# Layer B's attention: in every second unit the twelve products of the output projection move ahead of the unit's value products

## Chip, cores and metric

The kernel runs on one core of one Trainium2 chip. The metric is device microseconds of one execution, as a median over runs; a profile is one further execution, recorded by the hardware profiler.

## What is computed

The reference is a two-layer decoder trunk on x of shape (1, 2048, 1024) in float32. Layer A is causal attention with forget gates. Layer B, which the change touches, is a sliding-window attention over keys and values that are shared by groups of heads, followed by a gate and an output projection:

```python
q, gate = jnp.split(u @ w_in_b[j], [WIDTH_B], axis=-1)
q = partial_rope(rmsnorm(q.reshape(b, s, N_Q_HEADS_B, HEAD_DIM), qnorm_b_g[j]), positions)
o = swa_sink_attention(q, k_shared, v_shared, sinks[j]).reshape(b, s, WIDTH_B)
h = h + (o * jax.nn.silu(gate)) @ w_out_b[j]
```

In `swa_sink_attention` each block of 128 queries sees its own and the previous block of 128 keys through a band mask, with one learned sink logit per head in the softmax. There are 16 query heads and 4 key/value heads, so 4 query heads share one.

## The kernel before

Each float32 matrix product is made of products of high and low parts, three for a projection (high by high, high by low, low by high).

`attention_b` cuts the attention into 64 units: 16 blocks of 128 queries, and in each block the 4 key/value heads g = 0 to 3. A unit passes through a software pipeline, one stage per step n of the loop `for n in range(N + V_LAG_B)`:

- *scores*, of unit n: eight products (L1302) into one of two PSUM tiles b2. VectorE lays the mask over them (L1314), puts in the sink (L1315) and takes the maxima (L1318, tile nm); ScalarE makes the exponentials and their sums (L1321, four per unit, tile st).
- *norm_weights*, of unit n - 1: VectorE's reciprocal (L1330), GpSimd's multiplication (L1331).
- *weights_t*, of unit n - 3: four transposes on TensorE (L349) into the one PSUM tile fl; ScalarE copies the high part (L1346), VectorE makes the residue (L1347), and GpSimd masks both (L1350). The results lie in two buffers by turns.
- *differences*, once a block, when n % 4 is 1: GpSimd subtracts the previous block's values from the block's (L1360, L1362), ScalarE makes the high part (L1364), GpSimd the residue (L1365).
- *values*, of unit n - 4: four products (L1381) into one of two PSUM tiles pa; ScalarE copies the lower half (L1388, tile wr), VectorE adds twice (L1391) and multiplies by the gate (L1395), then ScalarE makes the high part (L1397) and VectorE the residue (L1398). These two are one operand of the output projection.

The output projection (`project`) is a generator that issues one product (L1451) at each call. A half block is 128 rows by 512 columns: 24 products into the single PSUM tile pb, then VectorE adds the residual (L1457) and SyncE stores it (L1458). There are 32 half blocks, 768 products, and the loop takes 12 of them per unit, 8 units behind the scores: so a half block begins in an even unit and is complete at the end of an odd one. `feed` takes them in portions, six ahead of *values* and six after it. In the first units of this part the weights of the projection are split as well (L1431 on ScalarE, L1432 on VectorE).

The order in which the code issues the steps is not kept as written: a scheduler places the instructions on each engine, and it has a different result on ScalarE, VectorE, GpSimd and SyncE when the order of the calls changes. On every engine instructions then run in the order of its queue, and a wait holds everything behind it. SyncE's queue holds all the loads and stores: the block's keys (L1276, L1279), queries (L1275), values (L1288), gates (L1292), and the residual's rows for each half block (L1446).

The main loop of the pipeline is printed here with the functions around it.

Of the kernel before, what the change touches and what calls it, by code (L numbers as in the profile page):

```python
# [77 lines left out]
O_LAG_B = 8  # L78
# [6 lines left out]
FEED_2 = 6  # L85
# [66 lines left out]
class Trunk:  # L152
# [1103 lines left out]
    def attention_b(self, w_out, res, dst):  # L1256
# [27 lines left out]
        def load_v(i):  # L1284

            ts_ = slice(i * P, (i + 1) * P)
            v = self.sb(("qn", "qn", "rows")[i % 3], [P, NKV, P], F32R)
            nc.sync.dma_start(  # L1288
                out=f_(v), in_=d["vb"][:, ts_, :].rearrange("g t e -> t g e")
            )  # L1290
            g = yg[:, 2 + i % 2, :].rearrange("p (c t) -> p c t", t=P)
            nc.sync.dma_start(out=g, in_=d["gtb"][:, ts_].rearrange("(c p) t -> p c t", p=P))  # L1292
            blk[i][3:5] = v, g

        def scores(u):
            i, g = units[u]
            ka, k2, qa, _, _, w = blk[i]

            ps = self.ps("b2", [P, G, 2 * P])
            for h in range(G):  # L1300
                for j, k in enumerate((ka, k2)):
                    nc.tensor.matmul(  # L1302
                        ps[:, h, 2 * P - w :], qa[:, g * G + h, :], k[:, g, :w],
                        start=j == 0, stop=j == 1,
                    )


            lg = ps[:, :, P:]
            if i == 0:
                m = self.band[:, 0].unsqueeze(1).to_broadcast([P, G, P])  # L1310
                nc.vector.tensor_tensor(lg, lg, m, ALU.add)
            else:
                m = self.band[:, 1].bitcast(I16).unsqueeze(1).to_broadcast([P, G, P])
                nc.vector.copy_predicated(lg, m, ps[:, :, :P])  # L1314
            nc.vector.tensor_copy(ps[:, :, P - 1], self.sink[:, g * G : (g + 1) * G])  # L1315
            lg = ps[:, :, P - 1 :]
            nm, rs = (self.sb(x, [P, G], bufs=6) for x in ("nm", "rs"))
            nc.vector.tensor_reduce(nm, lg, AX.X, ALU.max, negate=True)  # L1318
            pf = self.sb("st", [P, G, P + 1])
            for h in range(G):  # L1320
                nc.scalar.activation(  # L1321
                    pf[:, h], lg[:, h], AF.Exp, bias=nm[:, h : h + 1],
                    accum_out=rs[:, h : h + 1],
                )
            st[u] = pf[:, :, 1:], rs

        def norm_weights(u):

            pf, rs = st[u]
            self.tc.keep_in_program_order(nc.vector.reciprocal(rs, rs))  # L1330
            nc.gpsimd.tensor_tensor(  # L1331
                pf, pf, rs.unsqueeze(2).to_broadcast([P, G, P]), ALU.mult
            )
            st[u] = pf

        def weights_t(u):


            i, g = units[u]
            pf = st[u]  # L1340
            ps = self.ps("fl", [P, G, P])
            for h in range(G):
                self.flip(ps[:, h, :], pf[:, h])
            both, own = (php[:, u % 2, k] for k in range(2))
            ph, pl = (both[:, k] for k in range(2))
            nc.scalar.copy(ph, ps)  # L1346
            nc.vector.tensor_tensor(pl, ps, f_(ph), ALU.subtract)  # L1347
            if i:
                tri = self.tri.unsqueeze(1).to_broadcast([P, 2 * G, P])
                nc.gpsimd.tensor_tensor(  # L1350
                    own.rearrange("p k h q -> p (k h) q"),
                    f_(both).rearrange("p k h q -> p (k h) q"), tri, ALU.mult,
                )
            st[u] = (ph, pl, own[:, 0], own[:, 1])

        def differences(i):

            v, before = f_(blk[i][3]), f_(blk[i - 1][3])
            t = self.sb("wl", [P, NKV, P])
            nc.gpsimd.tensor_tensor(t, v, before, ALU.subtract)  # L1360
            t_ = t[:, :, :HD]
            nc.gpsimd.tensor_tensor(t_, t_, t[:, :, HD:], ALU.add)  # L1362
            dv = self.sb("wh", [P, NKV, P], F32R)
            nc.scalar.copy(dv[:, :, :HD], t_)  # L1364
            nc.gpsimd.tensor_tensor(dv[:, :, HD:], t_, f_(dv[:, :, :HD]), ALU.subtract)  # L1365
            dvs[i] = dv

        def values(u):


            i, g = units[u]
            ph, pl, oh, ol = st.pop(u)
            if i:
                v, dv = blk[i - 1][3], dvs[i]
                terms = ((v, ph), (v, pl), (dv, oh), (dv, ol))
            else:
                v = blk[i][3]
                terms = ((v, ph), (v, pl))
            pv = self.ps("pa", [P, G, P])
            for n_, (v, src) in enumerate(terms):  # L1380
                nc.tensor.matmul(  # L1381
                    pv.rearrange("p h q -> p (h q)"), v[:, g, :],
                    src.rearrange("p h q -> p (h q)"),
                    start=n_ == 0, stop=n_ == len(terms) - 1,
                )

            cr = self.sb("wr", [HD, G, P])
            nc.scalar.copy(cr, pv[HD:])  # L1388
            y = pv[:, 1::2, :]
            for s in (1, 0):  # L1390
                nc.vector.tensor_tensor(  # L1391
                    y[s * HD : (s + 1) * HD], pv[:HD, s::2, :], cr[:, s::2, :], ALU.add
                )
            pr = slice(g * G // 2, (g + 1) * G // 2)
            nc.vector.tensor_tensor(y, y, blk[i][4][:, pr, :], ALU.mult)  # L1395
            yh, yl = (yt(i, k, pr) for k in range(2))
            nc.scalar.copy(yh, y)  # L1397
            nc.vector.tensor_tensor(yl, y, f_(yh), ALU.subtract)  # L1398
# [16 lines left out]
        def weight_load(j):  # L1415
            half, t = 1 - j // 4, j % 4 * 2
            raws[j] = self.sb("wr", [P, 2, CH])
            nc.sync.dma_start(
                out=raws[j],
                in_=w_out[t * P : (t + 2) * P, half * CH : (half + 1) * CH].rearrange(  # L1420
                    "(k p) c -> p k c", p=P
                ),
            )

        def weight_split(j):
            half, t = 1 - j // 4, j % 4 * 2
            if t % 4 == 0:
                W[half][t // 4] = self.sb("big", [P, 2, 4, CH], F32R)
            h, lo = (W[half][t // 4][:, k, t % 4 : t % 4 + 2, :] for k in range(2))
            raw = raws.pop(j)  # L1430
            nc.scalar.copy(h, raw)  # L1431
            nc.vector.tensor_tensor(lo, raw, f_(h), ALU.subtract)  # L1432
# [30 lines left out]
        def feed(n):  # L1463
            nonlocal fed
            while fed < min(n, total):
                next(filler, None)
                fed += 1

        per = total // N
        for n in range(N + V_LAG_B):  # L1470
            if n < N:
                scores(n)
            if 0 < n <= N:
                norm_weights(n - 1)
            if n == T_LAG_B:
                php = self.sb("big", [P, 2, 2, 2, G, P], F32R)
            if n == V_LAG_B + NKV:
                odd += [[self.sb(t, [P, 4, P], F32R) for _ in range(2)] for t in ("wh", "wl")]
            if 0 <= n - B_SPLIT_AT < NDT:
                weight_split(n - B_SPLIT_AT)  # L1480
            if 0 <= n + 1 - B_SPLIT_AT < NDT:
                weight_load(n + 1 - B_SPLIT_AT)
            o = (n - O_LAG_B) * per
            feed(o + FEED_1)
            if n % NKV == 1 and NKV < n < N:
                differences(n // NKV)
            if 0 <= n - T_LAG_B < N:
                weights_t(n - T_LAG_B)
            feed(o + FEED_2)
            if 0 <= n - V_LAG_B < N:  # L1490
                values(n - V_LAG_B)
            feed(o + per)
            if n < N:
                i, g = units[n]
                if g == NKV - 2 and i + 1 < NTB:
                    load(i + 1)
                if g == NKV - 1 and i + 1 < NTB:
                    load_v(i + 1)
            yield
# [121 lines left out]
```

## Time and profile before

| | us |
|---|---|
| median of 3 runs | 2443.16 |
| lowest, highest | 2442.53, 2444.26 |
| profiled execution, its time | 2441.85 |
| profiled execution, span from the first to the last instruction | 2440.1 |

| engine | busy us | share of the span |
|---|---|---|
| TensorE (PE) | 2408.3 | 99% |
| TensorE's weight loads (PEld) | 2025.6 | 83% |
| VectorE (DVE) | 1728.7 | 71% |
| ScalarE (ACT) | 1258.6 | 52% |
| GpSimd (POOL) | 998.5 | 41% |

TensorE ran at a granted clock of 0.999. In layer B's attention, from about 2117 us to the end, the rows of the profile name a line of the kernel, an engine, an operation and its tiles, output before inputs ("pb<-big" is written to pb and reads big). An idle time in square brackets stands with what ended it. Matmul records are given with a modelled end, so on TensorE the distance from one start to the next is the surer measure.

### The profile page before, as it was taken

How to read it: one execution, taken by the hardware profiler on the slowest of the kernel's cores; microseconds unless marked ns; L12 is line 12 of the kernel's file. 1: busy time of each engine (PE TensorE's matmuls, PEld its weight loads, DVE VectorE, ACT ScalarE, POOL GpSimd, SP SyncE). 2: the span in 40 equal slices, each digit the busy share in tenths (PEclk: the TensorE clock that was granted, in tenths of full speed). 3: DMA queues.
4: the chain of work that ended last, by engine and by line, in shares of the span. 5: the costliest groups of instructions: out<-in, count | busy, mean ns of one | idle time of the engine just before them, and what ended most of it. 6: DMA issues, size and time to landing. Idle time of an engine off the chain costs nothing.

```text
span 2440.1 us, 36268 instructions
## 1 busy us (share of the span) xinstructions
PE 2408.3 (99%) x11952; PEld 2025.6 (83%) x11952; DVE 1728.7 (71%) x4098; ACT 1258.6 (52%) x2504; POOL 998.5 (41%) x643
## 2 busy tenths in 40 slices
PE   8999999999999999999999999999999999999999
PEld 6788899987888788878888878888888888888887
DVE  7656667735989888888888866556666523777776
ACT  5433324323878778777877761135422312555554
POOL 0000000011878777777778862200011000377775
PEclk9999999999999999999999999999999999999999
DMA  5656555677654755566465649975433415555552
GB/s 182 208 167 183 157 154 168 197 232 236 173 167 128 204 159 148 148 195 177 131 183 175 176 139 310 294 247 163 126 92 116 138 65 166 177 178 181 178 181 74
DMA packets 351516, 419.24 MB, mean 172 GB/s; under 512 B 64928, under 2 KB 248256, under 8 KB 345152
## 3 DMA queue, kind: packets, MB, share of 16 engines
q1 hardware_dynamic: 351328, 416.92, 57.2%
q8 instruction: 95, 1.56, 0.3%
q14 instruction: 93, 0.76, 0.1%
HBM read 265.29 MB, written 151.40 MB: 171 GB/s over the span
## 4 chain that ended last, share of the span: by engine, by line
PE 86%; DVE 4%; DMA 4%; ACT 2%; issue 1%; POOL 1%; SPq 1%; ACTq 0%; DVEq 0%; POOLq 0%
PE b L759 27%; PE pa L1021 10%; PE pb L1061 7%; PE b L1238 5%; PE sc L979 5%; PE sc L978 5%; PE pb L1451 5%; PE mx L933 5%; PE pb L722 3%; PE b L722 3%; PE pa L1381 2%; PE b L1302 2%; DMA wr<-wg 1%; PE pa L349 1%; PE pb L349 1%
## 5 line engine op out<-in xcount | busy, mean ns | idle before, releaser
L759 PE MATMUL b<-wh,big 128*128 128x512 f32 (+3 forms) x2560 | 774.4, 375 | 8.9 <-ACT wh L486 8.5
L997 POOL TENSOR_TENSOR big<-st,big 128x1024 fp32r<-128x1024 f32 (+1 forms) x320 | 655.3, 2067 | 246.4 <-ACT big L996 154.9
L759 PEld LDWEIGHTS b<-wh,big 128*128 128x128 f32 x2560 | 472.3, 189 | 81.3 <-ACT wh L486 10.7
L759 PE MATMUL b<-wl,big 128*128 128x512 f32 (+3 forms) x1280 | 475.0, 371 | 1.7 <-DVE wl L487 1.6
L1006 DVE TENSOR_TENSOR ac<-ac,st 128x512 f32<-128x512 f32 (+3 forms) x576 | 352.3, 612 | 55.1 <-ACT st L993 29.3
L993 ACT ACTIVATE st<-sc 128x512 f32<-128x512 f32 (+1 forms) x512 | 273.1, 582 | 127.5 <-PE sc L979 59.5
L1021 PE MATMUL pa<-big 128*128 128x512 f32 (+3 forms) x1280 | 318.7, 365 | 1.0 <-POOL big L997 1.0
L996 ACT CAST big<-st 128x1024 fp32r<-128x1024 f32 (+1 forms) x320 | 295.2, 923 | 8.3
L759 PEld LDWEIGHTS b<-wl,big 128*128 128x128 f32 x1280 | 242.0, 189 | 37.8 <-DVE wl L487 5.5
L1021 PEld LDWEIGHTS pa<-big 128*128 128x128 f32 x1280 | 229.5, 190 | 40.4 <-POOL big L997 3.0
L946 DVE TENSOR_REDUCE mt<-mx 128x1 f32<-128x384 f32 (+1 forms) x360 | 213.9, 597 | 30.5 <-PE mx L933 28.3
L495 ACT ACTIVATE sq<-b,r 128x512 f32<-128x512 f32 (+2 forms) x128 | 77.7, 607 | 302.5 <-PE b L759 299.6
L978 PE MATMUL sc<-big 128*128 128x512 f32 (+3 forms) x640 | 232.8, 368 | 0.1
L979 PE MATMUL sc<-big 67*128 67x512 f32 (+3 forms) x640 | 229.4, 367 | 0.0
L933 PE MATMUL mx<-big 66*128 66x512 f32 (+2 forms) x600 | 224.6, 379 | 0.2
L1061 PE MATMUL pb<-wh,wr 128*128 128x512 f32 x488 | 178.8, 399 | 6.7 <-DMA wr<-wg 6.7
L497 DVE TENSOR_REDUCE sm<-sq 128x8 f32<-128x512 f32 (+2 forms) x128 | 74.9, 585 | 139.4 <-ACT sq L495 139.2
L859 POOL MEMSET rot<- 128x512 bf16 x1 | 0.5, 524 | 421.5 <-PE pb L349 421.5
L1350 POOL TENSOR_TENSOR big<-big,tri 128x1024 fp32r<-128x1024 f32 x60 | 143.8, 2397 | 67.4 <-DVE big L1347 62.5
L941 DVE CUSTOM_DVE_ANT_0 mx<-mx,rot 128x384 f32<-128x384 f32 (+2 forms) x240 | 146.8, 616 | 19.4 <-PE mx L933 18.4
L978 PEld LDWEIGHTS sc<-big 128*128 128x128 f32 x640 | 121.9, 190 | 21.6 <-DVE st L542 0.5
L979 PEld LDWEIGHTS sc<-big 67*128 67x128 f32 x640 | 122.1, 191 | 19.4
(281 smaller groups left out, 4120.5 us busy)
## 6 DMA issues: line engine op xcount, KB each, us to landing
wr<-wg SPq DMA_DIRECT2D x62, 512.0 KB
va<-st SPq DMA_DIRECT2D x32, 512.0 KB
ka<-st SPq DMA_DIRECT2D x64, 256.0 KB
ut<-big SPq DMA_DIRECT2D x16, 1024.0 KB
big<-ka SPq DMA_DIRECT2D x16, 1024.0 KB
big<-qa SPq DMA_DIRECT2D x16, 1024.0 KB
qb<-st SPq DMA_DIRECT2D x64, 256.0 KB
big<-qb SPq DMA_DIRECT2D x16, 1024.0 KB
```

The source lines that it names most:

```text
L759: nc.tensor.matmul(ps[:, :n], u[tb // 4][:, dt, us], W[k][dt], start=(dt == 0 and i == 0), stop=(dt == NDT - 1 and i == 2),)
L933: mm = nc.tensor.matmul(ps, qb[:66, i * P : (i + 1) * P], kb[:66, k0:k1], start=True, stop=True,)
L941: nc.vector.tensor_tensor_reduce(out=ps, in0=ps, in1=mask_m[:, 512 - w :], scale=1.0, scalar=NEG, op0=ALU.add, op1=ALU.max, accum_out=f_(o),)
L946: nc.vector.reduce_max(o, ps, axis=AX.X)
L978: nc.tensor.matmul(o, ka[:, ks], qa[:, qs], start=not (last and n_), stop=False)
L979: nc.tensor.matmul(o, kb[:, ks], qb[:, qs], start=False, stop=not diag)
L993: nc.scalar.activation(pf[:, off : off + w], ps[:, :w], AF.Exp, scale=HD**-0.5)
L996: nc.scalar.copy(ph[:, :tw], pf[:, :tw])
L997: nc.gpsimd.tensor_tensor(pl[:, :tw], pf[:, :tw], f_(ph[:, :tw]), ALU.subtract)
L1006: nc.vector.tensor_tensor(a_, a_, pf[:, off : off + w], ALU.add)
L1021: nc.tensor.matmul(pv[:, q0 : q0 + w], v[:, k, :], src[:, off : off + w], start=(p == 0 and n_ == 0 and i == 0), stop=(last and n_ == 1 an ...
L1061: nc.tensor.matmul(ps, w[:, dt // 2 % 2, wk, dt % 2, :], us[dt][uk], start=(dt == 0 and i == 0), stop=(dt == NDT - 1 and i == 2),)
```

## The change

In odd units (those that complete a half block) the second portion is fed whole, ahead of `values`; the call behind `values` then has nothing left to issue. In even units nothing is altered. The number of products and their order among themselves stay the same.

```diff
@@ -1486,7 +1486,7 @@
                 differences(n // NKV)
             if 0 <= n - T_LAG_B < N:
                 weights_t(n - T_LAG_B)
-            feed(o + FEED_2)
+            feed(o + (per if (n - O_LAG_B) % 2 else FEED_2))
             if 0 <= n - V_LAG_B < N:
                 values(n - V_LAG_B)
             feed(o + per)
```

`per` is 12, `FEED_2` is 6, `O_LAG_B` is 8. What it does to the order on three engines follows; a minus stands before what was there, a plus before what is there now.

TensorE, in an odd unit of the steady part: scores, transposes, projection (pb), value products (pa), and the next unit's scores.

```order
 L1302 MATMUL b_21565<-big 128x256 x8
 L349 MATMUL fl<-ident,st 128x128 x4
-L1451 MATMUL pb<-big 128x512 x6
+L1451 MATMUL pb<-big 128x512 x12
 L1381 MATMUL pa<-big,rows 128x512 x2
 L1381 MATMUL pa<-big,wh 128x512 x2
-L1451 MATMUL pb<-big 128x512 x6
 L1302 MATMUL b_21626<-big 128x256 x8
```

The last six products of the half block have changed places with the four value products. From the third block of the projection to the last the order on VectorE and ScalarE is the same as before.

ScalarE, in the first units of the projection, where the weights are split (L1431): copies of value sums (L1388), exponentials (L1321), copies of transposed weights (L1346), high parts (L1397, L1364).

```order
 L1346 CAST big<-fl 128x512
 L1397 CAST wh<-pa 128x256
-L1388 COPY wr<-pa 64x512
 L1321 ACTIVATE st,rs<-b_21086,nm 128x129 x4
 L1364 CAST wh<-wl 128x4x64
+L1388 COPY wr<-pa 64x512
 L1431 CAST big<-wr 128x1024
-L1397 CAST wh<-pa 128x256
-L1346 CAST big<-fl 128x512
 L1321 ACTIVATE st,rs<-b_21151,nm 128x129 x4
-L1388 COPY wr<-pa 64x512
+L1346 CAST big<-fl 128x512
```

The copy L1388 has moved behind L1364, and the copy of the transposed weights (L1346) behind the next four exponentials. On VectorE the addition L1457 of the first half block has moved ahead of a sum L1391 in these units, and on GpSimd the differences of the next block (L1360, L1362) stand one L1350 earlier.

SyncE, in a steady block, before:

```order
L1276 DMA big<-kb 128x4x256
L1275 DMA big<-qb 128x16x128
L1288 DMA rows<-vb 128x4x128
L1458 DMA out_h<-sq 128x512
L1279 DMA big<-kb 64x4x256
L1292 DMA big<-gtb 128x8x128
```

and with the change:

```order
L1276 DMA big<-kb 128x4x256
L1275 DMA big<-qb 128x16x128
L1458 DMA out_h<-sq 128x512
L1288 DMA rows<-vb 128x4x128
L1279 DMA big<-kb 64x4x256
L1292 DMA big<-gtb 128x8x128
```

The store of a half block (L1458) has moved ahead of the load of a block of values (L1288), once a block.

## The prediction

> **What bounds the kernel now.** The page comes first. It has TensorE (PE) busy for nearly the whole span.
>
> ```profile
> span 2440.1 us, 36268 instructions
> PE 2408.3 (99%) x11952; PEld 2025.6 (83%) x11952; DVE 1728.7 (71%) x4098; ACT 1258.6 (52%) x2504; POOL 998.5 (41%) x643
> ```
>
> The profiled execution took 2441.85 us by the results, so 1.75 us lie outside its span. The runs shown have a median of 2443.16 us. I sum changes against 2441.85 and carry them over to the median.
>
> The change touches layer B's attention only, from about 2117 us on. The wait of PE there that the change seems aimed at (us in total, times, longest):
>
> ```profile
> PE pb L1451 <- DVE sq L1457: 3.3, 10, 1.1
> ```
>
> Bank pb exists once, each half block of the output projection fills it with 24 products, and the next half may not begin before VectorE's addition (L1457) has emptied it. The timeline of PE shows its size, start by start (us, duration):
>
> ```profile
> 2162.17 1.64 PE L1451 MATMUL pb<-big 128*128 128x512 f32 x6
> 2182.48 0.72 PE L1451 MATMUL pb<-big,wh 128*128 128x512 f32 x2
> ...
> 2253.33 1.12 PE L1302 MATMUL b<-big 128*128 128x256 f32 x8
> 2254.29 0.60 PE L349 MATMUL fl<-ident,st 128*128 128x128 f32 x4
> 2255.05 1.65 PE L1451 MATMUL pb<-big 128*128 128x512 f32 x6 [0.16 <-DVE sq L1457]
> ...
> 2259.76 0.60 PE L349 MATMUL fl<-ident,st 128*128 128x128 f32 x4
> 2260.11 1.64 PE L1451 MATMUL pb<-big 128*128 128x512 f32 x6
> 2261.59 0.62 PE L1381 MATMUL pa<-big,qn 128*128 128x512 f32 x2
> 2262.05 0.62 PE L1381 MATMUL pa<-big,wh 128*128 128x512 f32 x2
> ...
> 2275.78 0.72 PE L1451 MATMUL pb<-big,wh 128*128 128x512 f32 x2 [0.24 <-DVE sq L1457]
> ```
>
> From the transposes (L349) to the first product of pb (L1451) it takes 0.35 us undisturbed (2259.76 to 2260.11) and 0.76 with a wait (2254.29 to 2255.05). So a wait of 0.16 in the row costs 0.41, the row's 3.3 us of ten waits are about 3.3 + 10 x 0.25 = 5.8 us, and no more than that is to be had from this bank. Four units without a wait take 20.31 us (2162.17 to 2182.48), and four with one take 20.73 (2255.05 to 2275.78). A product takes 0.23 us (two from 2261.59 to 2262.05).
>
> Whether the 5.8 us can be had depends on why L1457 is late. These are the longest waits of the other engines from 2200 to 2400 us, some ten blocks of four units:
>
> ```profile
> ACT st L1321 <- DVE nm L1318: 28.3, 20, 1.8
> ACT wh L1364 <- POOL wl L1362: 17.5, 10, 2.2
> DVE pa L1391 <- ACT wr L1388: 23.8, 19, 1.5
> DVE sq L1457 <- PE pb L1451: 4.6, 11, 0.7
> POOL big L1350 <- DVE big L1347: 41.0, 37, 1.5
> ```
>
> VectorE (DVE), ScalarE (ACT) and GpSimd (POOL) wait for one another. Only one row has PE as the releaser. The timeline of the three, over one block:
>
> ```profile
> 2253.65 0.69 DVE L1318 TENSOR_REDUCE nm<-b 128x4 f32<-128x516 f32 x1
> 2254.37 0.37 ACT L1321 ACTIVATE st<-b,nm 128x129 f32<-128x129 f32 x1 [1.43 <-DVE nm L1318]
> 2254.33 0.66 DVE L1457 TENSOR_TENSOR sq<-pb,sq 128x512 f32<-128x512 f32 x1
> ...
> 2264.06 0.69 DVE L1457 TENSOR_TENSOR sq<-pb,sq 128x512 f32<-128x512 f32 x1 [0.35 <-PE pb L1451]
> 2265.19 0.58 ACT L1388 COPY wr<-pa 64x512 f32<-64x512 f32 x1
> 2265.80 0.43 DVE L1391 TENSOR_TENSOR pa<-pa,wr 64x256 f32<-64x256 f32 x1 [1.05 <-ACT wr L1388]
> ...
> 2268.02 2.40 POOL L1350 TENSOR_TENSOR big<-big,tri 128x1024 fp32r<-128x1024 f32 x1 [1.53 <-DVE big L1347]
> 2270.38 1.28 POOL L1360 TENSOR_TENSOR wl<-qn,rows 128x512 f32<-128x512 f32 x1
> ...
> 2274.38 0.69 DVE L1318 TENSOR_REDUCE nm<-b 128x4 f32<-128x516 f32 x1
> ```
>
> The L1457 for which PE stalled ran at 2254.33, right behind its predecessors on VectorE and with no wait for PE: the bank's last product stands ahead of the scores of 2253.33, a full microsecond earlier. VectorE was late, not PE. Its lateness runs in a ring: maximum L1318, exponentials on ACT, ACT's copy L1388, VectorE's sums L1391, its residue L1347, GpSimd's L1350 and value differences (L1360, L1362), ACT's L1364 and L1397, VectorE again. L1457 hangs on it as a side branch. One turn takes 2274.38 - 2253.65 = 20.73 us, just PE's period with a wait. So the ring sets the pace here, 0.42 us a block slower than PE's own 20.31, and PE's wait is where the difference shows. The one L1457 of the block that does wait for PE (2264.06, 0.35 us) holds nothing up, since the next instruction waits for ACT until 2265.80 anyway.
>
> **The change, term by term.** (1) *The wait for pb in the steady blocks.* In a completing (odd) unit six products change places with four value products, so the bank is full four products earlier, 4 x 0.23 = 0.92 us. The order on VectorE and ScalarE is the same as before there, so in the unit that stalls L1457 still follows L1318 and runs when the ring gets to it; PE reaches its next pb product after the same amount of work. Gain 0, with 5.8 us as the upper end if I misread the ring. In the other odd unit L1457's 0.35 us go, which nothing uses.
>
> (2) *The value products, later by six products* (6 x 0.23 = 1.4 us). ACT's L1388 waits for them. In the tighter of the two odd units they end by 2262.67 (2262.05 + 0.62) and ACT takes them at 2265.19. 2.5 us of cover against 1.4: nothing. If the cover were gone, each block would cost up to 1.4 us.
>
> (3) *SyncE's queue.* The store of the half block (L1458) now stands ahead of the load of the next values (L1288), which itself waits for the later value products.
>
> ```profile
> 2262.29 1.19 SPq L1288 DMA_DIRECT2D qn<-vb  x1
> 2264.78 0.51 SPq L1458 DMA_DIRECT2D out_h<-sq  x1
> ...
> 2124.86 1.58 POOL L1360 TENSOR_TENSOR wl<-rows,qn 128x512 f32<-128x512 f32 x1 [0.66 <-DMA rows<-vb]
> ...
> GB/s 0 33 63 139 381 356 332 321 313 339 350 353 358 341 380 368 224 48 62 110 270 347 295 159 258 135 4 0 0 16 0 0 0 303 221 0 0 53 217 234
> ```
>
> L1288 would be issued near 2264.8 instead of 2262.29, behind an L1458 that can itself be 0.35 us earlier. Its user is L1360 at 2270.38, a member of the ring. The last row has the traffic of 2260 to 2280 in half microseconds: the queue is full with the block's query load until 2268 and then falls, so the values land soon after 2268 either way. Cost 0. L1279, L1292 and the next L1446 stand behind L1288 and move with it; L1292 waited for VectorE's L1395 before and still does. The Trainium skill (DMA: Bandwidth & Descriptors, Anatomy of one DMA) gives a DMA a fixed cost of about 2.0 us besides its bytes; by that estimate the values would land before 2268, and no run here has yet shown the later issue.
>
> (4) *The first blocks.* Here the scheduler did reorder ACT, VectorE and GpSimd, among the splits of the weights (L1431, L1432).
>
> ```profile
> 2129.44 1.65 PE L1451 MATMUL pb<-big 128*128 128x512 f32 x6 [1.11 <-DVE sq L1457]
> 2135.52 0.63 PE L349 MATMUL fl<-ident,st 128*128 128x128 f32 x4 [1.21 <-DVE big L1347]
> ...
> 2133.01 0.59 ACT L1346 CAST big<-fl 128x512 fp32r<-128x512 f32 x1
> 2134.69 0.69 DVE L1347 TENSOR_TENSOR big<-fl,big 128x512 fp32r<-128x512 f32 x1
> ...
> 2162.51 0.59 ACT L1346 CAST big<-fl 128x512 fp32r<-128x512 f32 x1 [0.49 <-PE fl L349]
> ```
>
> L1457 now stands one sum ahead on VectorE, so PE's 1.11 us shrinks by about 0.4. But on ACT one copy (0.58 by the row of 2265.19) and four exponentials (4 x 0.37 by that of 2254.37) now precede the L1346 of 2133.01, and one cast of some 0.3 no longer does: it moves to about 2134.8, L1347 from 2134.69 to about 2135.45, and PE's transposes of 2135.52, which wait for it, to about 2136.2. Following the new orders on with the same durations, PE gets back some 0.4 and is 0.3 us late by 2147. The block's differences come out earlier on GpSimd, which puts the ring about 1 us ahead; that is worth nothing, as the ring still has to wait for PE until 2162.51. Taken: +0.3, between -1.4 (the first wait goes whole, 1.11 + 0.25) and +1.5 (the 1.21 doubles).
>
> (5) *The tail.* The last rows:
>
> ```profile
> 2409.50 0.71 PE L1381 MATMUL pa<-big,rows 128*128 128x512 f32 x2
> 2410.10 1.65 PE L1451 MATMUL pb<-big 128*128 128x512 f32 x6
> ...
> 2423.49 0.62 PE L1381 MATMUL pa<-big,wh 128*128 128x512 f32 x2
> 2427.08 0.42 DVE L1398 TENSOR_TENSOR wl<-pa,wh 128x256 fp32r<-128x256 f32 x1 [0.44 <-ACT wh L1397]
> ```
>
> Two products from 2409.50 on would end at 2409.96; the next began at 2410.10, 0.14 late, and the value products of two units are split around others. The new order has neither: -0.2. The last value products (2423.49 on) now have 18 instead of 24 products, 18 x 0.23 = 4.1 us, between them and the first product that needs their result. That result took from 2424.1 to 2427.5, 3.4 us: covered by 0.7. Bounds -0.4 to +0.6.
>
> **Sum.** 0 + 0 + 0 + 0.3 - 0.2 = +0.1 us on 2441.85; on the median about 2443.2. With the bounds of (4) and (5), 2441.4 to 2445.3.
>
> **Rivals.** *The bank was the cause.* PE waits for L1457 in the profile and is 99% busy; were L1457 late only because the bank fills late, 0.92 us would cover all steady waits of 0.41, and 5.8 us go: 2437.4. The Trainium skill says so much in Perfetto Trace Analysis, Identifying the Most-Contended Engine: optimize the engine with the highest occupancy, and look for what blocks it. By that rule TensorE's waits would be the prize; the trace speaks against the rule here, with PE at 99% and yet waiting 0.4 us a block for an engine at 71%. Against the rival: L1457 starts behind VectorE's own work, and the ring turns in 20.73 us without PE.
>
> *Only the early waits go.* The 1.36 and the 1.21 us of the first blocks both vanish, and the ring starts that much sooner: 2443.2 - 2.6 = 2440.6. For: they are the largest waits. Against: the ACT order above.
>
> *Slower: the values come late.* If a load of values takes longer than 2270.38 - 2264.8 = 5.6 us from its issue, GpSimd waits, and in the ring that counts in full in each of some 12 blocks. The profile has such a wait of 0.66 us at 2124.86, amid the weight loads. One of 0.6 us a block would give 2443.2 + 7.2 = 2450.4. Against: the traffic falls at 2268.
>
> That the change doesn't do what it says is ruled out by the order on PE.
>
> **How the numbers follow.** No change, 0.79; the bank, 0.06; the early waits alone, 0.08; late values, 0.07. Other than 0.2% (4.9 us, about what a measurement of this kernel can tell from none) needs the first or the last of the rivals: faster 0.06, slower 0.07, same 0.87. The range takes in the early waits and the bounds of (4) and (5) with the runs' own spread: 2440.2 to 2446.0.
>
> **What would show it.** Right: the waits of PE for L1457 between 2200 and 2400 us stay near ten of 0.2 us, a block still takes 20.73, and VectorE's wait for pb falls below 4.6 us. Wrong: four units in 20.31 us with PE's wait gone (the bank), or L1360 waiting for a DMA in each block (the values), or L1391 waiting longer for L1388 because of PE (term 2). A block longer than 20.8 us would say that the ring includes a step I took for covered.

## The result and the profile after

| | us |
|---|---|
| before, median of 14 runs | 2442.61 (2437.8 to 2445.53) |
| with the change, median of 14 runs | 2446.22 (2442.4 to 2451.62) |
| ratio, 95% interval | 1.0016 (1.0010 to 1.0023) |
| profiled execution with the change, its time | 2449.73 |
| its span | 2447.7 |

The change makes the kernel 2.4 to 5.6 us slower. The two profiled executions lie further apart than the medians, 7.6 us by their spans. TensorE's order is the same in both up to the transposes of step n = 9 (2122.68 us before, 2124.12 after), so 1.4 us of the 7.6 were there ahead of the first changed instruction. The other 6.2 are the change's and chance's: 5.0 us arise in the next 75 us, 1.1 in the rest (each rounded).

The page has TensorE as busy as before:

```profile
span 2447.7 us, 36263 instructions
PE 2410.1 (98%) x11952; PEld 2026.8 (83%) x11952; DVE 1728.7 (71%) x4098; ACT 1259.7 (51%) x2504; POOL 999.5 (41%) x643
```

Its 2410.1 us of busy time are 1.8 more than before, though the products are the same; the clock will account for them. The steady blocks came as forecast. The waits from 2200 to 2400 us, of the kernel after:

```profile
DVE pa L1391 <- ACT wr L1388: 30.5, 20, 1.5
ACT st L1321 <- DVE nm L1318: 26.8, 19, 1.8
...
ACT wh L1364 <- POOL wl L1362: 16.4, 9, 2.4
...
PE pb L1451 <- DVE sq L1457: 2.9, 9, 0.5
POOL wl L1360 <- DMA qn<-vb: 0.8, 2, 0.4
POOL wl L1360 <- DMA rows<-vb: 0.7, 1, 0.7
```

The row of PE's wait in the same stretch before:

```profile
PE pb L1451 <- DVE sq L1457: 2.2, 9, 0.5
```

VectorE's wait for the bank (L1457 for pb, 4.6 us before) is gone: the bank is full earlier. PE's wait for L1457 is not: nine times, 2.9 us, and 2.2 us before. VectorE's timeline of the kernel after has the turn of the ring:

```profile
2261.37 0.69 DVE L1318 TENSOR_REDUCE nm<-b 128x4 f32<-128x516 f32 x1
2262.05 0.66 DVE L1457 TENSOR_TENSOR sq<-pb,sq 128x512 f32<-128x512 f32 x1
...
2282.12 0.69 DVE L1318 TENSOR_REDUCE nm<-b 128x4 f32<-128x516 f32 x1
2282.81 0.66 DVE L1457 TENSOR_TENSOR sq<-pb,sq 128x512 f32<-128x512 f32 x1
```

A block takes 2282.12 - 2261.37 = 20.75 us, as before. Two blocks take longer, 21.25 and 21.49 us by the starts of L1360 (2214.61, 2235.86, 2257.35), and in both the values come late. New are the three waits of GpSimd's L1360 for a load of values. SyncE's queue and GpSimd at one of them:

```profile
2246.51 0.93 SPq L1275 DMA_DIRECT2D big<-qb  x1
2250.56 1.92 SPq L1458 DMA_DIRECT2D out_h<-sq  x1
2252.58 0.38 SPq L1288 DMA_DIRECT2D rows<-vb  x1
```

```profile
2235.86 1.30 POOL L1360 TENSOR_TENSOR wl<-qn 128x512 f32<-128x512 f32 x1 [0.44 <-DMA qn<-vb]
2257.35 1.29 POOL L1360 TENSOR_TENSOR wl<-rows,qn 128x512 f32<-128x512 f32 x1 [0.68 <-DMA rows<-vb]
2278.11 1.28 POOL L1360 TENSOR_TENSOR wl<-qn,rows 128x512 f32<-128x512 f32 x1
```

The store now stands ahead of the load, and here its issue alone took 1.92 us. L1360 stands 5.6 us behind the load's issue in the blocks without a wait (8.1 before the change), and in most blocks the values land within that. The load of 2229.75 took longer, 6.1 us to the L1360 of 2235.86. The load of 2252.58 landed within 4.8 us, but had itself been issued late, behind the store.

The larger part lies in the first blocks. TensorE there, of the kernel after:

```profile
2124.12 0.60 PE L349 MATMUL fl<-ident,st 128*128 128x128 f32 x4
2124.48 3.00 PE L1451 MATMUL pb<-big 128*128 128x512 f32 x12
...
2130.63 0.63 PE L349 MATMUL fl<-ident,st 128*128 128x128 f32 x4 [1.29 <-DVE big L1347]
2132.13 2.18 PE L1451 MATMUL pb<-big 128*128 128x512 f32 x6 [0.88 <-DVE sq L1457]
2134.11 1.05 PE L1381 MATMUL pa<-big,qn 128*128 128x512 f32 x2
...
2140.05 0.63 PE L349 MATMUL fl<-ident,st 128*128 128x128 f32 x4 [1.45 <-DVE big L1347]
...
2146.17 1.45 PE L1451 MATMUL pb<-big 128*128 128x512 f32 x5 [1.29 <-DVE big L1432]
```

Before the change PE waited here twice, 1.11 and 1.21 us. Now it waits four times in this profile, and between 2132 and 2137 its instructions are slow: two value products take 1.05 us instead of 0.62. The windows of the same stretch give the reason (from:to, length, busy time of PE, PEld, DVE, ACT and POOL, granted clock of PE, DMA):

```profile
2128.00:2132.00 4.00, 1.96 (x14) 1.51 (x12) 3.97 (x10) 1.15 (x5) 1.44 (x1) 1.00 0.60 196
2132.00:2136.00 4.00, 3.87 (x11) 3.06 (x12) 1.84 (x5) 2.28 (x9) 3.35 (x4) 0.63 0.36 128
2136.00:2140.00 4.00, 2.60 (x15) 2.10 (x13) 3.42 (x7) 3.55 (x12) 1.05 (x2) 0.94 0.13 24
```

The granted clock fell: 4 x (1 - 0.63) + 4 x (1 - 0.94) = 1.7 us of PE's time lost. In the profile of before it stays at 1.00 from 2124 to 2148. Whether this lengthened the kernel is settled below.

Who is late for the transposes of 2140.05? ScalarE and then VectorE of the kernel after, in the order in which they release each other:

```profile
2134.65 0.40 ACT L1364 CAST wh<-wl 128x256 fp32r<-128x256 f32 x1 [1.69 <-POOL wl L1362]
2135.08 0.58 ACT L1388 COPY wr<-pa 64x512 f32<-64x512 f32 x1
```

```profile
2135.69 0.43 DVE L1391 TENSOR_TENSOR pa<-pa,wr 64x256 f32<-64x256 f32 x1 [2.09 <-ACT wr L1388]
...
2136.64 1.75 DVE L1432 TENSOR_TENSOR big<-wr,big 128x1024 fp32r<-128x1024 f32 x1 [0.45 <-ACT big L1431]
...
2139.23 0.68 DVE L1347 TENSOR_TENSOR big<-fl,big 128x512 fp32r<-128x512 f32 x1
```

The same two instructions of ScalarE and VectorE's L1391 before the change:

```profile
2127.10 0.58 ACT L1388 COPY wr<-pa 64x512 f32<-64x512 f32 x1
...
2131.49 0.41 ACT L1364 CAST wh<-wl 128x256 fp32r<-128x256 f32 x1 [1.69 <-POOL wl L1362]
```

```profile
2128.37 0.43 DVE L1391 TENSOR_TENSOR pa<-pa,wr 64x256 f32<-64x256 f32 x1
```

L1364 waited the same 1.69 us for GpSimd then, but the copy L1388 had run ahead of it. The change moved the copy behind L1364, and it now waits with it. VectorE has L1391 next in its queue and stands still for 2.09 us; the split L1432 and the residue L1347, which frees the bank fl for the transposes, come after it.

### The profile page after: what moved, and what is told of

It reads as the page before. It is cut to its first block, busy times and chain, and to the rows that moved or that the text cites. A ratio compares the mean times of both kernels' runs of the same rounds, so it can differ in the third digit from the quotient of the medians.

```text
span 2447.7 us, 36263 instructions
## 1 busy us (share of the span) xinstructions
PE 2410.1 (98%) x11952; PEld 2026.8 (83%) x11952; DVE 1728.7 (71%) x4098; ACT 1259.7 (51%) x2504; POOL 999.5 (41%) x643
## 4 chain that ended last, share of the span: by engine, by line
PE 82%; DVE 6%; DMA 4%; ACT 4%; POOL 2%; issue 2%; SPq 0%; ACTq 0%; DVEq 0%; POOLq 0%
PE b L759 28%; PE pa L1021 10%; PE pb L1061 7%; PE b L1238 5%; PE sc L978 5%; PE sc L979 5%; PE mx L933 5%; PE pb L722 3%; PE pb L1451 3%; PE b L722 3%; DMA wr<-wg 1%; POOL big L1350 1%; PE pb L349 1%; PE pa L349 1%; PE pa L1238 1%
## 5 line engine op out<-in xcount | busy, mean ns | idle before, releaser
L1350 POOL TENSOR_TENSOR big<-big,tri 128x1024 fp32r<-128x1024 f32 x60 | 143.7, 2396 | 73.1 <-DVE big L1347 68.2
```

What stands on the lines that cost most here:

```text
L1350: nc.gpsimd.tensor_tensor(own.rearrange("p k h q -> p (k h) q"), f_(both).rearrange("p k h q -> p (k h) q"), tri, ALU.mult,)
```

## The experiments

The theory: the loss is made in the first blocks, by the place of L1388 behind L1364. The rivals: the late value loads make all of it; the twelve products' place on TensorE makes it; and, for the steady blocks, the bank and not the ring makes PE's wait. The table has, for every kernel, the ratio to the runs of before that were made beside it, and from its profile how much later than in the profile of before PE reaches the transposes of step 23 (2197.51 us there) when both are counted from the transposes of step 9 (*first blocks*), what the rest to the end adds (*rest*), and PE's time lost to a lower clock from 2124 to 2148.

| kernel | median us, before beside it | ratio (95%) | first blocks | rest | clock |
|---|---|---|---|---|---|
| whole change | 2446.22, 2442.61 | 1.0016 (1.0010 to 1.0023) | +5.0 | +1.1 | 1.7 |
| 1 late units | 2442.13, 2441.41 | 1.0004 (0.9995 to 1.0013) | 0.0 | -0.2 | 0 |
| 2 first units | 2445.14, 2441.41 | 1.0013 (1.0004 to 1.0022) | +3.9 | +0.1 | 1.7 |
| 3 first half only | 2444.02, 2441.41 | 1.0011 (1.0002 to 1.0020) | +2.1 | -0.3 | 1.7 |
| 4 second half only | 2442.46, 2441.41 | 1.0004 (0.9995 to 1.0013) | +0.3 | +1.1 | 0 |
| 5 differences behind | 2443.04, 2441.85 | 1.0003 (0.9993 to 1.0012) | +2.0 | +2.1 | 0 |
| 6 first half, differences behind | 2441.23, 2441.85 | 0.9994 (0.9985 to 1.0003) | +1.5 | 0.0 | 0 |
| 7 own copy buffers | 2446.84, 2441.85 | 1.0017 (1.0008 to 1.0026) | +2.0 | +0.1 | 0 |
| 8 one product more | 2442.59, 2441.85 | 1.0000 (0.9991 to 1.0009) | +1.1 | +0.9 | 0 |
| 9 order alone | 2443.24, 2441.78 | 1.0010 (1.0001 to 1.0019) | +4.0 | +0.2 | 0 |
| 10 L1364 on GpSimd | 2434.52, 2441.78 | 0.9973 (0.9964 to 0.9983) | +0.8 | -4.7 | 0 |
| 11 whole change, L1364 on GpSimd | 2437.47, 2441.78 | 0.9980 (0.9971 to 0.9989) | +0.7 | -3.4 | 0 |
| 12 as 6, L1364 on GpSimd | 2435.17, 2441.78 | 0.9973 (0.9963 to 0.9983) | +0.5 | -4.5 | 0 |

One piece of the column *first blocks* is not the change's. At the transposes of step 10 PE waits in some profiles because a load of the projection's weights landed late (ScalarE's L1431 waited 2.58 us for it in the profile after, 1.73 before, and the split L1432 behind it took 2.20 us beside GpSimd's L1360, 1.33 before). That cost 1.5 us in the profile of the whole change, 1.6 in kernel 2 and 1.6 in kernels 9 and 10, which feed as before, and nothing in the profile of before. Of the seven kernels with the first unit changed six show it (1.0 to 1.6 us), of the seven without it three (0.6 to 1.6). The order ahead of it is the same in the kernels before and after. Whether the change makes it likelier is left open.

Behind the landing the column divides again. From the transposes of step 10 to those of step 13 it takes 18.9 us before, 21.4 in the whole change and in kernels 2 and 9, and 21.2 in kernel 3: in this stretch the new order costs 2.3 to 2.5 us. The clock fell in three of these four profiles and not in kernel 9, which loses as much, so the fall costs nothing that shows. PE at the lower clock only waits less: 1.45 us for L1347 in the whole change, where the fall came first, and 3.07 in kernel 9. From step 13 to step 23 the whole change loses a further 1.0 us that kernels 2, 3 and 9 don't lose. Its profile has GpSimd's longest wait for a load of values just ahead of that (L1360, 2.82 us at 2149.83), but kernel 9 has one of 2.37 us there and loses nothing, so the cause of this 1.0 stays open.

A profile is one execution, and it scatters: from step 9 on kernel 5's profile is 4.1 us later than that of before, its median 1.2 us; kernel 7's 2.2, its median 5.0. Whether a kernel is slower is read from the medians, where it loses from the profiles.

### 1 to 4: which units make the loss

The four conditions in their order: late units, first units, first half only, second half only.

```diff
-            feed(o + (per if (n - O_LAG_B) % 2 else FEED_2))
+            feed(o + (per if n % 2 and n >= 16 else FEED_2))
+            feed(o + (per if n % 2 and n < 16 else FEED_2))
+            feed(o + (per if n % 4 == 1 else FEED_2))
+            feed(o + (per if n % 4 == 3 else FEED_2))
```

> The change is applied only from unit 16 on; the first units of the projection keep the order of before. Theory (the loss is made in the first blocks, about 5 us of the 6.2 by which the two profiles differ in this part, and 2 to 3 us of the 3.6 of the medians): the time is that of before plus at most 1.2 us for three late value loads, 2442.3 to 2444.3. Rival (the value loads, late behind the store in every block, make the whole loss): 2445 to 2447, with GpSimd waiting for a DMA at L1360 in several blocks. In both, a steady block takes 20.75 us and not 20.31.

> The change is applied only before unit 16 (the first two blocks of the projection); all later units are as before. Theory (first blocks): the loss of the whole change stays, 2445 to 2447.5, with the transposes about 3 to 5 us late by unit 20 and no wait of L1360 for a DMA after 2200 us. Rival (late values in every block): 2442 to 2443.5.

> The change is applied only in units with n % 4 = 1, in which no value load is issued; in the units with n % 4 = 3 the value load stays ahead of the store. Theory (first blocks, by the new order on ScalarE and VectorE among the splits of the weights): that order is as with the whole change, so 2444 to 2447. Rival (late values): the time of before, 2442 to 2443.5, no wait of L1360 for a DMA after 2200 us.

> The change is applied only in units with n % 4 = 3, where the value load comes behind the store. Theory (first blocks): 2442.3 to 2444.3, with some waits of L1360 for a DMA that cost about 1 us in all. Rival (late values): 2445 to 2447.

The kernels with the first completing unit changed (2 and 3) are slower with intervals above 1; those without it (1 and 4) can't be told from before. Kernel 1's median lies 0.2 us below the theory's range. Kernels 1 and 2 add up to about the whole: 0.0004 + 0.0013 against 0.0016. The late value loads alone are small: kernel 4 has one wait of L1360 of 1.2 us from 2180 to 2400 us and one of 0.3, and its rest is 1.1 us longer; in kernel 1, with the same order on SyncE in the steady blocks, one wait of 0.3 is all, and the rest is not longer. The rival is a part of the cause, not the whole.

In the profile of kernel 3 the weights landed in time, so the new order stands by itself:

```profile
2132.95 0.96 PE L349 MATMUL fl<-ident,st 128*128 128x128 f32 x4 [3.08 <-DVE big L1347]
```

PE's wait for L1347 has grown from 1.21 to 3.08 us, and right after it the clock falls.

### 5 and 6: ScalarE's order put back, TensorE's left

Kernel 5 is the whole change with one call moved; kernel 6 has the feeding of kernel 3 as well.

```diff
-            if n % NKV == 1 and NKV < n < N:
+            if n % NKV == 1 and NKV < n < N and n != 9:
                 differences(n // NKV)
...
                 values(n - V_LAG_B)
+            if n == 9:
+                differences(n // NKV)
```

> The whole change, and in unit 9 alone (the first that completes a half block) the value differences are written behind the value products instead of ahead of the transposes; by that ScalarE's copy L1388 stands ahead of L1364 again, as it did before the change, while TensorE's order stays that of the change. Theory (the early loss comes from L1388, which the change put behind L1364 and so behind GpSimd's L1362; VectorE's sums, splits and residues follow it, the transposes wait over 3 us and the clock then falls to half for some 3.5 us): the transposes that waited 3.2 us wait about 1.4 again, no clock of 0.5 between 2125 and 2150 us, and the time is that of before plus 0 to 1.5 (three late value loads): 2441.4 to 2443.2 beside a before of 2441.6. Rival (the products' new place on TensorE itself, or a late load of the weights, makes the loss whatever the order on ScalarE): 2444 to 2447, with the clock at 0.5.

> As the kernel with the differences behind in unit 9, but the twelve products stay ahead only in units with n % 4 = 1, so that the value loads keep their place ahead of the stores. Theory: both losses gone, what is left is the tail's gain of 0.2 us: 2440.8 to 2442.2 beside a before of 2441.6. Rival (bank: what was hidden by the losses now shows, up to 0.4 us a block): 2437 to 2440. Rival (the products' place on TensorE costs by itself): 2443.5 to 2445.

ScalarE of kernel 5:

```profile
2127.25 0.59 ACT L1388 COPY wr<-pa 64x512 f32<-64x512 f32 x1
2128.92 0.41 ACT L1364 CAST wh<-wl 128x256 fp32r<-128x256 f32 x1 [1.08 <-POOL wl L1362]
```

L1388 is free of L1364. PE's wait for L1347 is 1.79 us instead of 3.1 (1.4 was expected), the clock stays at 1.00, and both times lie where the theory had them. With twelve products ahead on TensorE in both, the rival that their place costs by itself falls as far as the medians can tell; from step 10 to 13 their profiles are 0.9 and 0.5 us longer than that of before, against 2.3 to 2.5 with L1388 behind L1364. Nor does kernel 6 show a gain from the bank that its interval would tell from none.

### 7: other buffers for the copies

```diff
-            cr = self.sb("wr", [HD, G, P])
+            cr = self.sb("wl", [HD, G, P])
```

> The kernel before the change, with the copies L1388 in buffers of their own (tag wl) instead of the two that they share with the loads of the projection's weights. The scheduler then puts L1388 behind L1364 in the first block with no change of TensorE's order. Theory (the place of L1388 behind L1364 makes the loss): the transposes wait 2.5 to 3.5 us there without the change, and the clock falls: 2443 to 2446 beside a before of 2441.6. Rival (the loss came from the weight loads, which wait for a buffer wr behind the late L1388): with buffers apart no loss, 2440 to 2442.

The time is above the theory's by 0.8 us and far from the rival's, but the profile doesn't show the wait that was expected: the transposes don't wait, PE waits for L1457 instead (1.39 us at 2130.83 and 1.28 at 2142.36). L1364 did hold ScalarE up for 2.70 us. The scheduler placed much else anew in this kernel, ahead of the first blocks too, so it settles only that a loss arises with separate buffers too. What sharing them costs in the whole change is read from its profile: L1431 waits 0.57 us for the weights at 2141.88, and VectorE takes up the split L1432 behind it at 2143.51 without a wait. Why kernel 7's median is 5.0 us above before, its profile only 2.2, is not known.

### 8: is TensorE the pace of a steady block?

```diff
+                            if i > 1 and nh == 0 and p == 1 and n_ == 2:
+                                for _ in range(1):
+                                    nc.tensor.matmul(
+                                        ps, yt(i, 1, slice(p, p + 1))[:, 0, :],
+                                        W[nh][p // 4][:, 1, p % 4, :], start=False, stop=False,
+                                    )
```

> The kernel before the change with one further product (low by low part, 0.23 us) a block of 128 rows from the third block on, 14 in all; the output gains that small term. Orders on the other engines stay. Theory (a ring of VectorE, ScalarE and GpSimd sets the pace of a steady block at 20.75 us, TensorE has 0.42 us to spare): the block still takes 20.75, only the two or three blocks outside the ring cost 0.23 each: 2441.7 to 2442.7 beside a before of 2441.6, and the waits of PE for L1457 shrink by about half. Rival (TensorE sets the pace and its wait for the bank is its own): 14 x 0.23 = 3.2 us more, 2444.8, a block of 20.98.

The file is six lines longer, so VectorE's addition L1457 is L1463 here.

```profile
2253.86 0.69 DVE L1318 TENSOR_REDUCE nm<-b 128x4 f32<-128x516 f32 x1
...
2274.64 0.68 DVE L1318 TENSOR_REDUCE nm<-b 128x4 f32<-128x516 f32 x1
```

```profile
PE pb L1451 <- DVE sq L1463: 0.7, 2, 0.4
```

A block takes 20.78 us with one product more, and the last row, of the waits from 2200 to 2400 us, has only two of PE's waits for the addition left: the product fills the time in which PE had waited. The median is 0.7 us over before, the ratio 1.0000. TensorE has time to spare in a steady block.

### 9: ScalarE's order changed, TensorE's feeding left

The kernel before, with the copy L1388 of one unit queued behind that block's L1364.

```diff
-            nc.scalar.copy(dv[:, :, :HD], t_)
+            dvs["c"] = nc.scalar.copy(dv[:, :, :HD], t_).ins
...
-            nc.scalar.copy(cr, pv[HD:])
+            with self.tc.issue_after(dvs["c"]) if u == 5 else ExitStack(): nc.scalar.copy(cr, pv[HD:])
```

> The kernel before the change, with one copy L1388 (of the first unit that completes a half block) made to stand behind that block's L1364 on ScalarE, as the change had put it; TensorE's feeding stays six and six. Theory (that place makes the early loss, not the products' place): VectorE's L1391 waits over 2 us for L1388 behind GpSimd's L1362, the transposes or the bank wait 2 to 3.5 us near 2130 us, in some executions the clock falls after it: 2443.5 to 2446.5 beside a before of 2441.7. Rival (the twelve products ahead make it, by where TensorE's waits then fall): the time of before, 2441 to 2442.5.

ScalarE, VectorE and TensorE of this kernel:

```profile
2131.29 0.41 ACT L1364 CAST wh<-wl 128x256 fp32r<-128x256 f32 x1 [1.70 <-POOL wl L1362]
2131.72 0.58 ACT L1388 COPY wr<-pa 64x512 f32<-64x512 f32 x1
```

```profile
2132.34 0.43 DVE L1391 TENSOR_TENSOR pa<-pa,wr 64x256 f32<-64x256 f32 x1 [2.11 <-ACT wr L1388]
```

```profile
2136.70 0.63 PE L349 MATMUL fl<-ident,st 128*128 128x128 f32 x4 [3.07 <-DVE big L1347]
...
2142.82 1.43 PE L1451 MATMUL pb<-big 128*128 128x512 f32 x5 [1.23 <-DVE big L1432]
```

The scheduler answered this one forced place with the changed kernel's order on ScalarE, VectorE and GpSimd in the first of these units. So the kernel shows what that order costs as a whole, without the products' place; that L1388 behind L1364 starts the loss is read from the chain of waits. Forced into this order, the kernel that feeds six and six shows the whole chain: 1.70, 2.11, 3.07, and 4.0 us in the first blocks, as in kernel 2, of which the late weights are 1.6 in both. The median is 0.3 us below the theory's range, and the ratio's interval lies above 1. The clock did not fall in this profile after the 3.07 us.

### 10 to 12: ScalarE out of the differences

```diff
-            nc.scalar.copy(dv[:, :, :HD], t_)
+            nc.gpsimd.tensor_copy(dv[:, :, :HD], t_)
```

Kernel 10 is the one before with this line, 11 the whole change with it, 12 kernel 6 with it.

> The kernel before the change, with the high part of the value differences (L1364) made by GpSimd instead of ScalarE; orders on TensorE and SyncE as before, nothing left out. Theory (a steady block's 20.75 us is a turn of the ring L1318, exponentials, L1388, L1391, L1347, L1350, L1360, L1362, L1364, L1397): without the step on ScalarE the ring is shorter by what L1364 waited (about 1.7 us a block), TensorE becomes the limit at 20.31, its waits for L1457 go: 10 to 12 blocks by 0.42, 4 to 5 us less, 2436.5 to 2438 beside a before of 2441.7. Rival (the bank pb, or something else than this ring, makes the wait): 2441 to 2442.5, a block of 20.73 as before.

> The whole change, with L1364 on GpSimd. Theory (L1388 has no L1364 to stand behind, the ring is out of the way): most of the early loss is gone; what is left against the kernel before with L1364 on GpSimd is the late value loads and the landing of the weights, 0 to 2 us: 2437 to 2439.5 beside a before of 2441.7. Rival (the place of the products makes the loss): 3 to 4 us more than the kernel before with L1364 on GpSimd. Rival (with the ring gone the bank shows and the change gains): less than that kernel by 1 us or more.

> Twelve products ahead only in units with n % 4 = 1, the differences behind the value products in unit 9, and L1364 on GpSimd: no early loss and no late value load. Theory: as the kernel before with L1364 on GpSimd, less the tail's 0.2: 2436.3 to 2438 beside a before of 2441.7. Rival (the place of the products costs by itself): 1.5 us more than that kernel.

TensorE's scores and VectorE's addition in kernel 10, and the waits from 2200 to 2400 us:

```profile
2254.38 1.12 PE L1302 MATMUL b<-big 128*128 128x256 f32 x8
...
2274.65 1.12 PE L1302 MATMUL b<-big 128*128 128x256 f32 x8
```

```profile
2259.66 0.69 DVE L1457 TENSOR_TENSOR sq<-pb,sq 128x512 f32<-128x512 f32 x1 [1.64 <-PE pb L1451]
```

```profile
DVE sq L1457 <- PE pb L1451: 30.9, 19, 1.6
ACT st L1321 <- DVE nm L1318: 27.2, 20, 1.4
...
DVE pa L1391 <- ACT wr L1388: 3.1, 18, 0.4
```

A block now takes 20.27 us, PE's own time, and PE's wait for L1457 is gone from the list: VectorE waits for PE there 19 times, up to 1.6 us. The ring is broken by moving one copy of 0.41 us off ScalarE. The median gains 7.3 us, more than the 4 to 5 that were expected; by the profile the steady blocks give 4.7, and the ratio's interval is 4.2 to 8.8 us, so the rest may be chance.

With L1364 out of ScalarE's queue the whole change costs little in the first blocks (kernel 11 against 10: 0.7 and 0.8, and 0.5 more when both are counted from step 10, behind the landing of the weights). What it still costs is the value loads: L1360 waits four times for a DMA in the steady part, once 2.35 us, and the rest is 1.3 us longer. By the medians 11 lies 3.0 us over 10. The bank's earlier filling brings nothing even where TensorE is the limit. Kernel 12, with the loads of values in their old place, equals 10; its median lies 1.1 us below the theory's range. Kernels 10 and 12 beat both the kernel before and the change.

## Why the prediction missed

**The ring: right.** Term (1) gave the steady wait for pb a gain of 0. A block still takes 20.75 us, PE still waits for L1457, and kernels 8 and 10 show the reason from both sides: a product more costs no block time, and a copy less on ScalarE gives PE's own 20.3. The upper end of 5.8 us was too high, as its row counted the 1.11 us of the first blocks too: the steady blocks' nine waits of 2.2 us are worth 2.2 + 9 x 0.25 = 4.5, and kernel 10 gained 4.7 there. The rival that the bank was the cause, at 2437.4, is refuted. The Trainium skill (Perfetto Trace Analysis, Identifying the Most-Contended Engine) has the engine of highest occupancy optimized first, with TensorE's headroom judged by its share of the peak rate and the busy share of its weight loads. The weight loads are busy for 83% here, above VectorE's 71%, so the rule would have chosen TensorE; in the trace TensorE's steady waits went when a copy left ScalarE, at 52%.

**The value products later (term 2): right in the steady blocks.** VectorE's wait for L1388 grew (23.8 to 30.5 us in all), but the block did not.

**SyncE's queue (term 3): taken at 0, measured +1.4 us in the profile of the change** (its rest of +1.1 and the tail's 0.3), +1.1 in kernel 4, +2.1 in kernel 5, +1.3 between kernels 10 and 11, nothing in kernel 1. The rival had the mechanism: values that come late stop GpSimd and throw the ring back. Its threshold of 5.6 us from issue to landing fits the longest waits from 2200 us on in kernels 4, 5 and 11 (6.3, 5.9 and 6.4 us) and one of the whole change's (6.1); at 2257.35 the load landed within 4.8 us, but had been issued late. The step that failed is "the values land soon after 2268 either way", read off one block. The fixed cost of 2.0 us that the prediction cites beside it is given in that section of the Trainium skill for DMAs that GpSimd issues; SyncE issued these, and the late ones took 4.8 to 6.4 us. In a few blocks the store or the load found the queue full and the load came later, so not each of some 12 blocks pays, nor none.

**The first blocks (term 4): the step that failed.** The prediction took +0.3, with an upper end of +1.5. From step 10 to step 13 the new order cost 2.3 to 2.5 us in the four profiles that have it. Of the +5.0 in the profile of the change this is 2.5; 1.5 is the chance landing of the weights, and 1.0 stays open. The reading of the orders was right, and so was the first wait (1.11 to 0.65 us in kernel 3, where the weights landed in time; 0.4 less was forecast). Wrong was the price of the moved copy: "on ACT one copy (0.58 by the row of 2265.19) and four exponentials (4 x 0.37 by that of 2254.37) now precede the L1346" adds up durations, and puts L1347 0.76 us later. But L1388 had moved behind L1364, and L1364 doesn't start when ScalarE is free; it starts when GpSimd has made L1362. The row for it was at hand: ScalarE's wait for L1362 was 17.5 us in ten blocks. Everything behind a waiting instruction waits with it, on ScalarE and then, through L1391, on VectorE (1.70 and 2.11 us in kernel 9). So L1347 came 1.4 to 1.7 us later, counted from step 10, and PE's wait for it became 3.1 us in kernels 2, 3 and 9. Then, where the prediction gives PE 0.4 back, it lost 0.9 more. The splits L1432 took 1.75 and 2.60 us, 1.20 and 1.65 before, as GpSimd's work now came first where the two overlap (below), and PE waited for the second of them (1.29 us in the whole change, 1.23 in kernel 9). PE's clock fell in three of the four profiles, 1.7 us of its time each, but that is no part of the loss.

**The tail (term 5): right in size.** From the transposes of step 59 to the end it takes 55.5 us before and 55.2 in kernel 1 and in the whole change; 0.2 less was forecast.

**The range.** 2440.2 to 2446.0 missed 2446.22 narrowly. That it was near is partly luck: the runs of before had a median 0.55 us lower this time. By the change itself the miss is wider, +0.1 and at most +2.1 forecast, 2.4 to 5.6 measured. An upper end for a moved instruction should have been the longest wait of the instruction that now stands ahead of it, 2.2 us by the row of L1364, passed on whole, plus the value rival's; both were in the text, one of them unpriced.

## What to carry to other kernels

When a change moves an instruction in an engine's queue, price it by when the instruction ahead of it can start, not by how long that takes: an instruction put behind one that waits for another engine inherits the wait, and so does the next engine. An engine at 99% that waits 0.4 us a block for a side branch is not helped by filling its bank earlier; find the ring whose turn is the block's time, and shorten that. A load that moves behind a store loses its cover in the worst block, not in the average one.

## What the runs showed of the hardware

**The clock after a wait.** Past the program's start, a fall of PE's granted clock to 0.5 followed eight of the nine waits above 3 us (near 1053 us after 3.37 to 4.09 us; here after 3.06 and 3.08, not after 3.07). It lasted 3.4 us (1.7 us of PE's time lost), and 6.8 in four of the profiles near 1053 us. Between 1.2 and 3 us it followed some: at 2132 us after 1.29 and 0.88 us close together, near 830 us after 1.24 and 1.25 in two profiles but not after 1.24 and 1.28 in two others, near 1365 us after 1.7 in four but not after 2.30 in one, near 1053 us after 2.69 to 2.85 in four but not after 2.95. The Trainium skill (TensorE: Matmul & The Clock Gate, What's actually happening) has the clock halved after an idle window of about 3.4 us whose start runs free of the program. The half clock, its length of one or two such windows and its run-to-run place agree with that; that waits of 1.2 to 2.9 us can bring it on is what the traces add.

**VectorE beside GpSimd.** The split L1432 and GpSimd's L1331 overlap in both profiles. Before the change VectorE started first:

```profile
2133.57 1.20 DVE L1432 TENSOR_TENSOR big<-wr,big 128x1024 fp32r<-128x1024 f32 x1
```

```profile
2133.74 1.93 POOL L1331 TENSOR_TENSOR st<-st,rs 128x512 f32<-128x512 f32 x1 [1.03 <-DVE rs L1330]
```

After it GpSimd started first, and L1432 (2136.64, shown above) took 1.75 us; the next split ran beside two instructions of GpSimd:

```profile
2136.27 1.04 POOL L1331 TENSOR_TENSOR st<-st,rs 128x512 f32<-128x512 f32 x1 [0.41 <-DVE rs L1330]
```

```profile
2143.51 2.60 DVE L1432 TENSOR_TENSOR big<-wr,big 128x1024 fp32r<-128x1024 f32 x1
```

The one that starts second pays: 0.9 us of GpSimd's time in the first case, 0.55 of VectorE's in the second. The Trainium skill (SBUF — State Buffer, Who interferes with whom) has a VectorE instruction with two SBUF inputs, as L1432 is, contend with a GpSimd instruction that reads SBUF, and the order of issue decide which of them blocks; the trace agrees. A changed order so moves time from one engine to the other with no instruction added.
